# Products with the values emitted a step behind the transposes, and one ring of four banks for scores and transposes

## The chip, the cores and the metric

The kernel runs on one core of a Trainium2 chip. The time is that of the device for one whole execution, in microseconds, and the measure of a version is the median of its runs.

## The reference, cut to what matters

One decoder block over 2048 tokens of width 1024, all in float32. A modulated RMS norm is followed by one input projection, whose columns feed two head groups: four heads of chunked gated linear attention (GLA) and four heads of differential attention. Both groups' outputs go through one output projection (`w_out`), a norm and a residual; then comes a squared-ReLU MLP of width 4096 with the same frame. The change lies around the differential attention, whose core is this:

```python
    for blk in range(seq // Q_BLOCK):                       # 128 queries a block
        s = jnp.einsum('bhmqd,bhmkd->bhmqk', qb, kb) * scale   # m: two maps a head
        p = jax.nn.softmax(jnp.where(mask, s, -jnp.inf), axis=-1)
        p_diff = p[:, :, 0] - lam * p[:, :, 1]
        outs.append(jnp.einsum('bhqk,bhkd->bhqd', p_diff, vf[:, :, :q1]))
    ...
    do = from_heads(rms_norm(do, diff_norm) * (1.0 - lambda_init))
    return jnp.concatenate([go, do], axis=-1) @ w_out
```

## The kernel before

**Stages.** From 0 to about 667 us the kernel computes the norm, the input projections and the GLA chunks. Attention over the first 1024 queries (tiles t = 0 and 1 of 512 tokens) runs from about 667 to 892 us, at first between the last projections; attention over t = 2 and 3 from about 897 to 1300 us, with the output projection between its steps. From about 1345 us to the end the MLP runs.

**A step of attention.** `attention` is a generator over steps (t, h, j): tile, head, block of 128 queries. A step has one tick (one `yield`) for each 512 keys, so t + 1 ticks. In a tick, `qk(cur, ci)` issues for both maps two matmuls into a PSUM bank S (L209), and VectorE moves each bank to SBUF while it keeps a running minimum (L214, or L217 for the masked block). After the ticks, `softmax(cur)` takes two exponentials on ScalarE (L227) and one combination of the two maps on VectorE (L233). Two steps later (`lag` 2) come, in the same ticks, the products with the values, `pv(old, ci)`: up to four transposes of P into a bank PT (L248), one copy of the bank to SBUF by ScalarE (L250), and the matmuls of the copy with V into the head's bank O (L252), two instructions for each block of keys. After a head's last step, `finish` takes the norm of O (squares L262 on ScalarE, L264 and L266 on VectorE), transposes the result into a bank `dps` (L269), splits it (L271, L272) and stores it to `mixS`.

**Banks.** PSUM has eight banks in this pool: two each for the tags A (projections, Y), B (scores S; GLA's `sps`), C (PT, `dps`, transposes of other parts) and D (O).

**What lies between.** `interleave` runs the output projection between ticks: 1.5 to 2 sub-steps of three matmuls Y (L873 to L875) for each tick, as far as the tokens' heads are in `finished`. `prep_first` prepares the MLP's first operands in the same way (`ntr`, L923). The weights `w_out` are loaded in eight pieces by POOL (L850) into the three slots of tag `wx`, and each is split into two by ScalarE (L853) and VectorE (L854), after two ticks of attention for each piece. The tokens' x (L866) use the same slots later.

**Order.** Each engine runs its instructions in an order that is settled when the program is built: a scheduler takes, of what its own model of time holds to be ready, that which comes first in the program. So instructions can stand ahead of others that the program has before them. K, V and q are loaded by SP (L185, L187, L197), up to two steps ahead.

Of the kernel before, what the change touches and what calls it, by code (L numbers as in the profile page):

```python
# [9 lines left out]
F32 = mybir.dt.float32  # L10
# [4 lines left out]
ALU = mybir.AluOpType  # L15
# [4 lines left out]
P = 128  # L20
S = 2048
D = 1024
NK = D // P
NH = 4
# [25 lines left out]
def tile_hybrid_block(  # L50
# [3 lines left out]
    nc = tc.nc  # L54
# [95 lines left out]
    def modulate(xts, a1, sh, hi, lo, tp, ttag, tb, pp, ptags):  # L150

        for k in range(NK):
            ps = pp.tile([P, 512], F32, tag=ptags[k % len(ptags)], name="ntr", bufs=2)
            for i in range(4):
                nc.tensor.transpose(ps[:, i * P:(i + 1) * P], xts[i][:, k * P:(k + 1) * P], ident)
            hf = tp.tile([P, 512], F32, tag=ttag, name="nhf", bufs=tb)
            nc.scalar.activation(hf, ps, AF.Identity, bias=sh[:, k:k + 1], scale=a1[:, k:k + 1])
            nc.vector.tensor_copy(hi[:, k, :], hf)
            eng = nc.gpsimd if k % 2 else nc.vector
            eng.tensor_tensor(lo[:, k, :], hf, hi[:, k, :].bitcast(F32), op=ALU.subtract)  # L160


    finished = set()


    def attention(tlist, sb, pw, pb, pp, tags, kb_, vb_, lag):
# [69 lines left out]
                rsd[t, h] = sb.tile([P, 4], F32, tag="rsd", name="rsd", bufs=3)  # L236
            nc.vector.tensor_copy(rsd[t, h][:, j:j + 1], sums[:, 1, 0:1])

        def pv(step, g):
            t, h, j = step  # L240
            pd, Vc = tiles[step][0][0], heads[t, h][1]
            if (t, h) not in outs:
                outs[t, h] = pp.tile([P, 4, P], F32, tag=tags["O"][0], name="O", bufs=tags["O"][1])
            nb = 4 * t + j + 1
            kbs = range(4 * g, min(4 * g + 4, nb))
            tp = pp.tile([P, 4, P], F32, tag=tags["T"][0], name="PT", bufs=tags["T"][1])
            for kb in kbs:
                nc.tensor.transpose(tp[:, kb % 4, :], pd[:, kb * P:(kb + 1) * P], ident)  # L248
            pt = sb.tile([P, 4, P], F32, tag="PTs", name="PTs", bufs=3)
            nc.scalar.copy(pt[:, 0:len(kbs), :], tp[:, 0:len(kbs), :])  # L250
            for kb in kbs:
                nc.tensor.matmul(outs[t, h][:, j, :], pt[:, kb % 4, :], Vc[g][:, kb % 4, :], start=(kb == 0),  # L252
                                 stop=(kb == nb - 1))

        def finish(t, h):

            finished.add((t, h))
            ops, rs1 = outs.pop((t, h)), rsd.pop((t, h))
            ss = sb.tile([P, 4], F32, tag="dss", name="dss", bufs=2)
            for j in range(4):  # L260
                junk = sb.tile([P, P], BF16, tag="djunk", name="djunk", bufs=1)
                nc.scalar.activation(junk, ops[:, j, :], AF.Square, scale=rs1[:, j:j + 1], accum_out=ss[:, j:j + 1])  # L262
            rr = rsqrt_col(sb, ss, 4, 1.0 / P, "dr")
            nc.vector.tensor_tensor(rr, rr, rs1, op=ALU.mult)  # L264
            on = sb.tile([P, 4, P], F32, tag="don", name="don", bufs=1)
            nc.vector.tensor_tensor(on, ops, rr.unsqueeze(2).broadcast_to([P, 4, P]), op=ALU.mult)  # L266
            gps = pp.tile([P, 4, P], F32, tag=tags["T"][0], name="dps", bufs=tags["T"][1])
            for j in range(4):
                nc.tensor.transpose(gps[:, j, :], on[:, j, :], ident)  # L269
            mo = sb.tile([P, 4, 2, P], F32R, tag="dmo", name="dmo", bufs=1)  # L270
            nc.scalar.activation(mo[:, :, 0, :], gps, AF.Copy, scale=gnc[:, 1:2])  # L271
            nc.vector.scalar_tensor_tensor(mo[:, :, 1, :], gps, gnc[:, 1:2], mo[:, :, 0, :].bitcast(F32),  # L272
                                           op0=ALU.mult, op1=ALU.subtract)
            nc.gpsimd.dma_start(mixS[t][:, :, NH + h, :, :], mo.bitcast(F32))

        n = len(steps)
        for s in range(n + lag):
            cur = steps[s] if s < n else None
            old = steps[s - lag] if s >= lag else None
            if cur is not None:  # L280
                for a in range(3):
                    load(steps[min(s + a, n - 1)])
                tiles[cur] = ([sb.tile([P, pw], F32, tag="P", name="P", bufs=pb) for _ in range(2)],
                              [sb.tile([P, 4], F32, tag="nm", name="nm", bufs=8) for _ in range(2)],
                              sb.tile([P, 2, 2], F32, tag="sums", name="sums", bufs=4))
            nq = cur[0] + 1 if cur is not None else 0
            np_ = old[0] + 1 if old is not None else 0
            for ci in range(max(nq, np_)):
                if ci < nq:
                    qk(cur, ci)  # L290
                if ci < np_:
                    pv(old, ci)
                yield
            if cur is not None:
                softmax(cur)
            if old is not None:
                del tiles[old]
                if old[2] == 3:
                    finish(old[0], old[1])

# [133 lines left out]
    run(sh_a, 3)  # L436
    xts = load_x(0)
    run(sh_a)
    norm_in(0, xts, "CBDCBDCB")

    def gla_consts(pool, lraw):

# [144 lines left out]
    def gla_mix(qd, kdT, AT, gv, state, tag):  # L587

        ops = pp.tile([P, NH, P], F32, tag=tag, name="ops", bufs=2)
        for j in range(2):  # L590
            for hh in range(2):
                nc.tensor.matmul(ops[:, 2 * j + hh, :], qd[j], state[:, j, hh, :], start=True, stop=False)
                nc.tensor.matmul(ops[:, 2 * j + hh, :], AT[:, j, hh, :],
                                 gv[:, (2 * j + hh) * P:(2 * j + hh + 1) * P], start=False, stop=True)
        ups = pp.tile([P, 2, 2, P], F32, tag="C", name="ups", bufs=2)
        for j in range(2):
            nc.tensor.matmul(ups[:, j, :, :], kdT[:, j * P:(j + 1) * P], gv[:, 256 * j:256 * j + 256],
                             start=True, stop=True)
        return ops, ups
# [11 lines left out]

    def gla_store(ck, onm, sog, pool):
        on, mf = onm[:, 0, :, :], onm[:, 1, :, :]
        gps = pp.tile([P, NH, P], F32, tag="C", name="gps", bufs=2)
        for h in range(NH):
            nc.tensor.transpose(gps[:, h, :], on[:, h, :], ident)
        nc.vector.scalar_tensor_tensor(mf, gps, gnc[:, 0:1], sog, op0=ALU.mult, op1=ALU.mult)
# [5 lines left out]
    def gla(ts2):  # L623

        states = glac[3]
        for ck in range(4 * ts2[0], 4 * ts2[0] + 8):
            t, ci = ck // 4, ck % 4
            cs = slice(ci * P, (ci + 1) * P)
            gv, sog = gla_in(ck, sg, 2)
            tps = pp.tile([P, 256], F32, tag="C", name="tps", bufs=2)  # L630
            for j in range(2):
                nc.tensor.transpose(tps[:, j * P:(j + 1) * P], Ei[t, j][:, cs], ident)
            kdT = sg.tile([P, 256], F32, tag="kdT", name="kdT", bufs=2)
# [1 line left out]

            AT = sg.tile([P, 2, 2, P], F32, tag="AT", name="AT", bufs=2)
            for hh in range(2):
                sps = pp.tile([P, 2, P], F32, tag="B", name="sps", bufs=2)
                r = slice(64 * hh, 64 * hh + 64)
                for j in range(2):  # L640
                    nc.tensor.matmul(sps[:, j, :], Ei[t, j][r, cs], E[t, j][r, cs], start=True, stop=True)
                nc.vector.tensor_tensor(AT[:, :, hh, :], sps, tri.unsqueeze(1).broadcast_to([P, 2, P]), op=ALU.mult)
# [13 lines left out]
    def gla_any(tq, gn, gcon, masks):  # L656
# [20 lines left out]
        for ck in range(4 * tq, 4 * tq + 4):  # L677
# [1 line left out]
            gv, sog = gla_in(ck, gn, 1)  # L679
            AT = gn.tile([P, 2, 2, P], F32, tag="AT", name="AT")  # L680
            kdT = gn.tile([P, 256], F32, tag="kdT", name="kdT")
            tps = pp.tile([P, 256], F32, tag="C", name="tps", bufs=2)
            qd, eb = [], []
            for j in range(2):
                b = b16s[j][:, cs]

                def scores(qq, kk, mask, first):
                    for hh in range(2):
                        r = slice(64 * hh, 64 * hh + 64)
                        sps = pp.tile([P, P], F32, tag="B", name="sps", bufs=2)  # L690
                        nc.tensor.matmul(sps, kk[r], qq[r], start=True, stop=True)
                        if first:
                            nc.vector.tensor_tensor(AT[:, j, hh, :], sps, mask, op=ALU.mult)
# [118 lines left out]

    cA = ExitStack()
    sa = cA.enter_context(tc.tile_pool(name="pA0", bufs=2, side="right", reuse_waits="tile"))
    atags = {"S": ("B", 2), "O": ("D", 2), "T": ("C", 2)}
    at = attention((0, 1), sa, 1024, 6, pp, atags, 3, 3, 2)
    while run(dp, 1):
        run(at, AT0)
# [24 lines left out]
    sw = c1.enter_context(tc.tile_pool(name="p1w", bufs=2, side="left", reuse_waits="tile"))  # L843
    gtg = sw.tile([P, D], F32, tag="gtg", name="gtg", bufs=1)
    nc.gpsimd.dma_start(gtg, gtS[0].partition_broadcast(P))
    wohi, wolo = [], []
    for k in range(NK):
        run(at, WL)
        raw = sw.tile([P, D], F32, tag="wx", name="woraw", bufs=3)
        nc.gpsimd.dma_start(raw, w_out[k * P:(k + 1) * P, :])  # L850
        wh = sw.tile([P, D], F32R, tag=f"wohi{k}", name="wohi", bufs=1)
        wl = sw.tile([P, D], F32R, tag=f"wolo{k}", name="wolo", bufs=1)
        nc.scalar.copy(wh, raw)  # L853
        nc.vector.tensor_tensor(wl, raw, wh.bitcast(F32), op=ALU.subtract)  # L854
        wohi.append(wh)
        wolo.append(wl)

    def out_proj(tiles):

        for tk in tiles:  # L860
# [6 lines left out]
            yps = []  # L867
            ss = sw.tile([P, 2], F32, tag="wss", name="wss", bufs=2)
            for b in range(2):
                yp = pp.tile([P, 512], F32, tag=("B" if tk > 12 and tk % 2 else "A"), name="Y", bufs=2)  # L870
                cs = slice(512 * b, 512 * b + 512)
                for k in range(NK):
                    nc.tensor.matmul(yp, mx[:, k, 0, :], wohi[k][:, cs], start=(k == 0), stop=False)  # L873
# [34 lines left out]
    def prep_first(pool, tag):  # L908


        for n in range(16):
# [5 lines left out]
                nc.gpsimd.dma_start(raw[:, j], xnS[0][:, 4 * j + i].rearrange("p (e k) c -> p e k c", e=2)[:, :, k, :])  # L917
            for _ in range(3):
                yield
            ps = pp.tile([P, 2, 2, P], F32, tag=tag, name="ntr", bufs=2)  # L920
            for e in range(2):
                for j in range(2):
                    nc.tensor.transpose(ps[:, e, j, :], raw[:, j, e, :], ident)  # L923
# [577 lines left out]
```

## Time and profile before

| | |
|---|---|
| median of 3 runs | 2619.75 us (2618.13 to 2629.93) |
| the profiled execution | 2620.44 us |
| its span | 2618.7 us |
| TensorE matmul busy / weight loads busy | 95% / 78% of the span |
| VectorE / ScalarE / GpSimd busy | 61% / 44% / 17% |
| mean granted TensorE clock | 0.982 of full speed |

The profiled execution is 0.69 us above the median, and 1.7 us of it lie outside the span. TensorE has two rows: PE is the matmuls, whose ends are modelled, so that consecutive ones overlap in the trace; PEld is the weight load ahead of each. An idle time is put down to what released the instruction after it. "PEld O L252 <- ACT PTs L250" reads: the weight load of line 252, for the bank O, stood until ScalarE's copy of line 250 was done.

### The profile page before, as it was taken

Reading aid. Unit: us, or ns where it says so; the run is one execution under the profiler, and the core shown is the slowest. Engines: PE = TensorE matmul, PEld = TensorE weight load, DVE = VectorE, ACT = ScalarE, POOL = GpSimd, SP = SyncE. Lnnn points to the kernel's source line nnn. Section 1 sums busy time; section 2 is a strip of 40 time slices with the busy share of each in tenths; the row PEclk is TensorE's granted clock in tenths of the full one; section 3 lists DMA queues with packets and bytes.
Section 4 is the critical chain, followed back from the end, with each engine's and each line's share of the span. In section 5 each row is a group of like instructions: output and inputs, shape, how many; then the busy total and the mean of one; then the engine's idle time right before and its main releaser. Section 6 shows DMA issues by size and latency. Waiting matters only on the chain.

```text
span 2618.7 us, 35437 instructions
## 1 busy us (share of the span) xinstructions
PE 2482.6 (95%) x12532; PEld 2043.2 (78%) x12532; DVE 1595.4 (61%) x3111; ACT 1154.8 (44%) x2185; POOL 435.5 (17%) x642
## 2 busy tenths in 40 slices
PE   3999999999998899999999999999999999999998
PEld 2887787987787787787877878788888888788886
DVE  5545765247764766766568666866665435443756
ACT  3351224323444655565546454655454324222444
POOL 1211332102320113223002231121121000100000
PEclk9999999999999899999999999999999999999999
DMA  6354552344744756565376564654447857755856
GB/s 235 107 193 137 170 196 77 125 131 155 224 155 142 227 173 207 186 201 187 109 261 234 194 238 141 225 190 144 139 151 258 289 189 234 268 197 162 282 168 208
DMA packets 219898, 491.63 MB, mean 188 GB/s; under 512 B 25872, under 2 KB 79936, under 8 KB 218176
## 3 DMA queue, kind: packets, MB, share of 16 engines
q1 hardware_dynamic: 171504, 329.33, 39.8%
q0 software_dynamic: 48208, 159.95, 16.3%
q8 instruction: 101, 1.65, 0.3%
q14 instruction: 85, 0.70, 0.1%
HBM read 329.79 MB, written 159.39 MB: 187 GB/s over the span
## 4 chain that ended last, share of the span: by engine, by line
PE 33%; issue 20%; DMA 5%; POOL 5%; DVE 3%; ACT 2%; SPq 0%; POOLq 0%; DVEq 0%; ACTq 0%
PE dn L1361 6%; PE dn L1363 6%; PE dn L1362 6%; PE O L252 3%; PE S L209 3%; PE Y L873 1%; PE Y L875 1%; POOL uS L1121 1%; PE Y L874 1%; POOL uS L1152 1%; PE PT L248 1%; DMA mx<-mixS 1%; PE upY L1195 1%; PE upY L1194 1%; PE upY L1193 1%
## 5 line engine op out<-in xcount | busy, mean ns | idle before, releaser
L1361 PE MATMUL dn<-dnhi,uhi 128*128 128x512 f32 x880 | 344.2, 391 | 4.8 <-DVE du L1339 4.7
L1363 PE MATMUL dn<-dnhi,ulo 128*128 128x512 f32 x880 | 343.8, 391 | 0.1
L1362 PE MATMUL dn<-dnlo,uhi 128*128 128x512 f32 x880 | 343.8, 391 | 0.0
L1285 ACT CAST uhi<-us 128x1024 fp32r<-128x1024 f32 (+1 forms) x126 | 118.7, 944 | 352.6 <-PE dn L1362 325.8
L1287 DVE TENSOR_TENSOR ulo<-us,uhi 128x1024 fp32r<-128x1024 f32 (+1 forms) x126 | 137.0, 1087 | 152.6 <-ACT uhi L1285 149.9
L209 PE MATMUL S<-K,q 128*128 128x512 f32 (+3 forms) x640 | 193.9, 402 | 14.2 <-DVE P L214 7.5
L488 PE MATMUL projt<-hThi,whi 128*128 128x512 f32 x512 | 206.3, 403 | 0.6 <-DVE cols L370 0.3
L489 PE MATMUL projt<-hTlo,whi 128*128 128x512 f32 x512 | 205.9, 402 | 0.0
L490 PE MATMUL projt<-hThi,wlo 128*128 128x512 f32 x512 | 201.8, 394 | 2.1 <-DVE wlo L425 2.1
L1361 PEld LDWEIGHTS dn<-dnhi,uhi 128*128 128x128 f32 x880 | 165.7, 188 | 41.0 <-issue 5.1
L1363 PEld LDWEIGHTS dn<-dnhi,ulo 128*128 128x128 f32 x880 | 165.7, 188 | 35.7 <-DVE ulo L1287 0.6
L1362 PEld LDWEIGHTS dn<-dnlo,uhi 128*128 128x128 f32 x880 | 165.7, 188 | 35.1
L227 ACT ACTIVATE P<-P,nm 128x128 f32<-128x128 f32 (+15 forms) x128 | 153.8, 1203 | 65.2 <-DVE nm L217 59.7
L1075 ACT CAST wuhi<-wA 128x512 fp32r<-128x512 f32 x160 | 99.1, 619 | 162.7 <-PE upV L1194 67.2
L252 PEld LDWEIGHTS O<-V,PTs 128*128 128x128 f32 x1088 | 136.5, 193 | 33.4 <-ACT PTs L250 26.6
L252 PE MATMUL O<-V,PTs 128*128 128x128 f32 x1088 | 154.7, 285 | 7.3 <-ACT PTs L250 3.5
L1195 PE MATMUL upY<-hhi,wulo 128*128 128x512 f32 x384 | 151.0, 393 | 1.5 <-DVE wulo L1076 1.5
L1193 PE MATMUL upY<-hhi,wuhi 128*128 128x512 f32 x384 | 150.9, 393 | 0.0
L1194 PE MATMUL upY<-hlo,wuhi 128*128 128x512 f32 x384 | 150.9, 393 | 0.0
L502 PE MATMUL projn<-whi,hThi 128*128 128x256 f32 x512 | 147.2, 288 | 3.8 <-DVE cols L370 2.3
L209 PEld LDWEIGHTS S<-K,q 128*128 128x128 f32 x640 | 111.7, 197 | 48.8 <-DVE P L214 21.9
L503 PE MATMUL projn<-wlo,hThi 128*128 128x256 f32 x512 | 146.7, 287 | 0.0
(321 smaller groups left out, 5759.9 us busy)
## 6 DMA issues: line engine op xcount, KB each, us to landing
us<-uS SPq DMA_DIRECT2D x94, 512.0 KB, 4.5
wA<-in_w_up_dram SPq DMA_DIRECT2D x128, 256.0 KB, 3.0
uS<-t POOLq DMA_DIRECT2D x128, 256.0 KB, 3.2
adaraw<-in_ada_w_dram SPq DMA_DIRECT2D x48, 512.0 KB, 4.4
wraw<-in_w_in_dram SPq DMA_DIRECT2D x48, 512.0 KB, 4.5
uS<-c POOLq DMA_DIRECT2D x96, 256.0 KB, 3.0
K<-kS SPq DMA_DIRECT2D x40, 512.0 KB, 4.6
wds<-in_w_down_dram SPq DMA_DIRECT2D x78, 256.0 KB, 4.3
```

The lines of the kernel that those rows point to most:

```text
L209: nc.tensor.matmul(ps[:, :wd], qt[:, m, hl, qs], Kc[ci][:, m, :wd], start=(hl == 0), stop=(hl == 1))
L227: nc.scalar.activation(Ps[m][:, :width], Ps[m][:, :width], AF.Exp, scale=-1.0, bias=nms[m][:, t:t + 1], accum_out=sums[:, 0, m:m + 1])
L252: nc.tensor.matmul(outs[t, h][:, j, :], pt[:, kb % 4, :], Vc[g][:, kb % 4, :], start=(kb == 0), stop=(kb == nb - 1))
L488: nc.tensor.matmul(ps, whi[k][:, cs], hi[:, k, :], start=(k == 0), stop=False)
L489: nc.tensor.matmul(ps, whi[k][:, cs], lo[:, k, :], start=False, stop=False)
L490: nc.tensor.matmul(ps, wlo[k][:, cs], hi[:, k, :], start=False, stop=(k == NK - 1))
L1193: nc.tensor.matmul(ps, whi[:, k, :], hi[:, k, :], start=(first and k == 0), stop=False, skip_group_check=not first)
L1194: nc.tensor.matmul(ps, whi[:, k, :], lo[:, k, :], start=False, stop=False, skip_group_check=not first)
L1195: nc.tensor.matmul(ps, wlo[:, k, :], hi[:, k, :], start=False, stop=(k == 3), skip_group_check=not first)
L1361: nc.tensor.matmul(banks[t], uhi[:, tk], whi, start=first, stop=False, skip_group_check=on)
L1362: nc.tensor.matmul(banks[t], uhi[:, tk], wlo, start=False, stop=False, skip_group_check=on)
L1363: nc.tensor.matmul(banks[t], ulo[:, tk], whi, start=False, stop=last, skip_group_check=on)
```

## The change

`pv` is taken apart. `turn` (transposes and copy) stays where `pv` was; the products are put into a list and emitted one tick later, between that tick's `qk` and `turn`. A head's norm follows its last product (`norm`), and `finish` (transposes, split, store) comes two ticks after that. When the steps are over, further ticks empty the list. The scores and the transposes share tag C, which now has four banks; tag B is gone, and what used it (GLA's `sps`, the norm's transposes at the start, some late Y) takes C. The first three pieces of `w_out` are loaded ahead of the loop, and piece k + 3 behind the split of piece k.

```diff
-        def pv(step, g):
+        queue, tick = [], [0]
+        def later(n_, f, *a):
+            queue.append((tick[0] + n_, f, a))
+        def due():
+            for e in [e for e in queue if e[0] <= tick[0]]:
+                queue.remove(e)
+                e[1](*e[2])
+        def turn(step, g):
             t, h, j = step
...
             nc.scalar.copy(pt[:, 0:len(kbs), :], tp[:, 0:len(kbs), :])
+            later(1, pv, step, g, kbs, pt, heads[t, h][1])
+
+        def pv(step, g, kbs, pt, Vc):
...
             for kb in kbs:
                 nc.tensor.matmul(outs[t, h][:, j, :], pt[:, kb % 4, :], Vc[g][:, kb % 4, :], start=(kb == 0),
                                  stop=(kb == nb - 1))
-        def finish(t, h):
-            finished.add((t, h))
+            if j == 3 and kbs[-1] == nb - 1:
+                norm(t, h)
+        def norm(t, h):
...
             nc.vector.tensor_tensor(on, ops, rr.unsqueeze(2).broadcast_to([P, 4, P]), op=ALU.mult)
+            later(2, finish, t, h, on)
+        def finish(t, h, on):
+            finished.add((t, h))
...
             for ci in range(max(nq, np_)):
+                tick[0] += 1
                 if ci < nq:
                     qk(cur, ci)
+                due()
                 if ci < np_:
-                    pv(old, ci)
+                    turn(old, ci)
                 yield
...
-                if old[2] == 3:
-                    finish(old[0], old[1])
+        while queue:
+            tick[0] += 1
+            due()
+            yield
...
-                sps = pp.tile([P, 2, P], F32, tag="B", name="sps", bufs=2)
+                sps = pp.tile([P, 2, P], F32, tag="C", name="sps", bufs=4)
...
-    atags = {"S": ("B", 2), "O": ("D", 2), "T": ("C", 2)}
+    atags = {"S": ("C", 4), "O": ("D", 2), "T": ("C", 4)}
...
+    def load_wo(k):
+        raw = sw.tile([P, D], F32, tag="wx", name="woraw", bufs=3)
+        nc.gpsimd.dma_start(raw, w_out[k * P:(k + 1) * P, :])
+        woraw.append(raw)
+    for k in range(3):
+        load_wo(k)
     for k in range(NK):
         run(at, WL)
-        raw = sw.tile([P, D], F32, tag="wx", name="woraw", bufs=3)
-        nc.gpsimd.dma_start(raw, w_out[k * P:(k + 1) * P, :])
...
+        if k + 3 < NK:
+            load_wo(k + 3)
```

## Rows read from the trace of the kernel before

**Rows 1.** The page's first part: busy time, share of the span, instructions.
```profile
PE 2482.6 (95%) x12532; PEld 2043.2 (78%) x12532; DVE 1595.4 (61%) x3111; ACT 1154.8 (44%) x2185; POOL 435.5 (17%) x642
```

**Rows 2.** Stretches of the attention: start and end, length, busy time of each engine (instructions), granted clock, share of the DMA engines, GB/s.
```profile
667.00:750.00 83.00, 78.81 (x422) 63.58 (x420) 66.13 (x206) 45.36 (x131) 23.13 (x29) 1.00 0.67 209
836.00:912.00 76.00, 61.16 (x300) 46.85 (x301) 51.82 (x148) 45.47 (x100) 11.96 (x18) 0.82 0.75 237
912.00:1000.00 88.00, 87.30 (x506) 71.33 (x504) 62.38 (x182) 48.76 (x105) 15.44 (x18) 1.00 0.54 176
1000.00:1100.00 100.00, 94.09 (x540) 75.41 (x540) 72.40 (x215) 58.44 (x121) 32.63 (x41) 1.00 0.62 201
1100.00:1200.00 100.00, 95.94 (x581) 80.43 (x581) 68.25 (x191) 57.49 (x108) 29.49 (x36) 0.97 0.61 197
1200.00:1293.00 93.00, 90.96 (x564) 76.00 (x563) 62.64 (x179) 55.94 (x106) 17.45 (x21) 1.00 0.41 133
```

**Rows 3.** Waits of the weight loads over the whole span: us in total, times, longest us.
```profile
PEld O L252 <- ACT PTs L250: 26.6, 87, 1.2
...
PEld S L209 <- DVE P L214: 21.9, 36, 2.4
...
PEld S L209 <- DVE nm L217: 12.2, 21, 3.0
...
PEld ops L593 <- DVE AT L642: 7.9, 9, 2.1
...
PEld dps L269 <- issue: 6.1, 7, 4.3
...
PEld dps L269 <- PE S L209: 2.4, 4, 0.9
```

**Rows 4.** Waits of the matmuls over the whole span, same columns.
```profile
PE Y L873 <- DMA mx<-mixS: 11.4, 2, 7.1
...
PE S L209 <- DVE P L214: 7.5, 12, 2.1
PE S L209 <- DVE nm L217: 5.6, 6, 2.6
PE dps L269 <- DVE don L266: 5.2, 3, 4.2
...
PE O L252 <- ACT PTs L250: 3.5, 10, 0.8
...
PE PT L248 <- DMA K<-kS: 0.5, 1, 0.5
```

**Rows 5.** Groups by line in 912 to 1293 us: line, engine, operation, out<-in, shapes, count; busy us, mean ns of one; idle us before them and what ended it.
```profile
L250 ACT COPY PTs<-PT 128x512 f32<-128x512 f32 (+2 forms) x108 | 56.6, 533 | 78.6 <-PE PT L248 78.5
L214 DVE TENSOR_SCALAR_CACHE_REDUCE P<-S,nm 128x512 f32<-128x512 f32 x92 | 67.5, 746 | 20.2 <-PE S L209 19.8
L233 DVE SCALAR_TENSOR_TENSOR P<-P,cf 128x1280 f32<-128x1280 f32 (+7 forms) x31 | 58.8, 1898 | 0.0
L227 ACT ACTIVATE P<-P,nm 128x1408 f32<-128x1408 f32 (+7 forms) x60 | 99.0, 1651 | 29.2 <-DVE nm L217 29.1
```

**Rows 6.** One wait of the products in order of time: start, us, engine, line, operation, count, in brackets the idle time before it and its releaser.
```profile
1079.11 0.63 PE L209 MATMUL S<-K,q 128*128 128x512 f32 x2
...
1079.84 0.56 ACT L250 COPY PTs<-PT 128x512 f32<-128x512 f32 x1
...
1080.45 0.97 PEld L252 LDWEIGHTS O<-V,PTs 128*128 128x128 f32 x8 [1.15 <-ACT PTs L250]
1080.45 1.16 PE L252 MATMUL O<-V,PTs 128*128 128x128 f32 x8 [0.71 <-ACT PTs L250]
```

**Rows 7.** One wait of the scores, same columns.
```profile
1095.31 2.08 DVE L233 SCALAR_TENSOR_TENSOR P<-P,cf 128x1792 f32<-128x1792 f32 x1
...
1095.58 0.50 PE L209 MATMUL S<-K,q 128*128 128x384 f32 x2
...
1097.38 0.74 DVE L214 TENSOR_SCALAR_CACHE_REDUCE P<-S,nm 128x512 f32<-128x512 f32 x1
...
1098.18 2.13 PE L209 MATMUL S<-K,q 128*128 128x384 f32 x5 [2.10 <-DVE P L214]
```

**Rows 8.** POOL's loads of `w_out` in order of time.
```profile
837.47 1.69 POOL L850 DMA_DIRECT2D woraw<-in_w_out_dram  x3 [0.35 <-PE S L209]
849.17 0.53 POOL L850 DMA_DIRECT2D woraw<-in_w_out_dram  x1 [10.01 <-DVE sums L230]
...
854.76 0.55 POOL L850 DMA_DIRECT2D woraw<-in_w_out_dram  x1 [2.20 <-DVE wolo L854]
859.41 0.53 POOL L850 DMA_DIRECT2D woraw<-in_w_out_dram  x1 [4.10 <-ACT PTs L250]
```

**Rows 9.** ScalarE's and VectorE's first and second split of `w_out`, in order of time.
```profile
846.57 1.04 ACT L853 CAST wohi<-woraw 128x1024 fp32r<-128x1024 f32 x1 [5.47 <-DMA woraw<-in_w_out_dram]
...
847.65 1.23 DVE L854 TENSOR_TENSOR wolo<-woraw,wohi 128x1024 fp32r<-128x1024 f32 x1 [4.91 <-ACT wohi L853]
...
853.25 1.22 DVE L854 TENSOR_TENSOR wolo<-woraw,wohi 128x1024 fp32r<-128x1024 f32 x1
```

**Rows 10.** A load queue's own waits, 660 to 1310 us: the V loads (L187) on products.
```profile
SPq L187 <- PE O L252: 74.6, 11, 22.8
```

More of the change, by code (lines that the diff above doesn't have):

```diff
@@ L152, in modulate @@
         for k in range(NK):
-            ps = pp.tile([P, 512], F32, tag=ptags[k % len(ptags)], name="ntr", bufs=2)
+            ps = pp.tile([P, 512], F32, tag=ptags[k % len(ptags)], name="ntr",
+                         bufs=4 if ptags[k % len(ptags)] == "C" else 2)
             for i in range(4):
@@ L237, in softmax @@
             nc.vector.tensor_copy(rsd[t, h][:, j:j + 1], sums[:, 1, 0:1])
-        def pv(step, g):
+        queue, tick = [], [0]
[6 more added lines that the diff above has]
+        def turn(step, g):
             t, h, j = step
-            pd, Vc = tiles[step][0][0], heads[t, h][1]
-            if (t, h) not in outs:
-                outs[t, h] = pp.tile([P, 4, P], F32, tag=tags["O"][0], name="O", bufs=tags["O"][1])
+            pd = tiles[step][0][0]
             nb = 4 * t + j + 1
@@ L250, in pv @@
             nc.scalar.copy(pt[:, 0:len(kbs), :], tp[:, 0:len(kbs), :])
+            later(1, pv, step, g, kbs, pt, heads[t, h][1])
+        def pv(step, g, kbs, pt, Vc):
+            t, h, j = step
+            nb = 4 * t + j + 1
+            if (t, h) not in outs:
+                outs[t, h] = pp.tile([P, 4, P], F32, tag=tags["O"][0], name="O", bufs=tags["O"][1])
             for kb in kbs:
@@ L438, in tile_hybrid_block @@
     run(sh_a)
-    norm_in(0, xts, "CBDCBDCB")
+    norm_in(0, xts, "CCDCCDCC")
     def gla_consts(pool, lraw):
@@ L594, in gla_mix @@
                                  gv[:, (2 * j + hh) * P:(2 * j + hh + 1) * P], start=False, stop=True)
-        ups = pp.tile([P, 2, 2, P], F32, tag="C", name="ups", bufs=2)
+        ups = pp.tile([P, 2, 2, P], F32, tag="C", name="ups", bufs=4)
         for j in range(2):
@@ L613, in gla_store @@
         on, mf = onm[:, 0, :, :], onm[:, 1, :, :]
-        gps = pp.tile([P, NH, P], F32, tag="C", name="gps", bufs=2)
+        gps = pp.tile([P, NH, P], F32, tag="C", name="gps", bufs=4)
         for h in range(NH):
@@ L629, in gla @@
             gv, sog = gla_in(ck, sg, 2)
-            tps = pp.tile([P, 256], F32, tag="C", name="tps", bufs=2)
+            tps = pp.tile([P, 256], F32, tag="C", name="tps", bufs=4)
             for j in range(2):
@@ L681, in gla_any @@
             kdT = gn.tile([P, 256], F32, tag="kdT", name="kdT")
-            tps = pp.tile([P, 256], F32, tag="C", name="tps", bufs=2)
+            tps = pp.tile([P, 256], F32, tag="C", name="tps", bufs=4)
             qd, eb = [], []
@@ L689, in scores @@
                         r = slice(64 * hh, 64 * hh + 64)
-                        sps = pp.tile([P, P], F32, tag="B", name="sps", bufs=2)
+                        sps = pp.tile([P, P], F32, tag="C", name="sps", bufs=4)
                         nc.tensor.matmul(sps, kk[r], qq[r], start=True, stop=True)
@@ L845, in tile_hybrid_block @@
     nc.gpsimd.dma_start(gtg, gtS[0].partition_broadcast(P))
-    wohi, wolo = [], []
+    wohi, wolo, woraw = [], [], []
+    def load_wo(k):
[4 more added lines that the diff above has]
+        load_wo(k)
     for k in range(NK):
         run(at, WL)
-        raw = sw.tile([P, D], F32, tag="wx", name="woraw", bufs=3)
-        nc.gpsimd.dma_start(raw, w_out[k * P:(k + 1) * P, :])
         wh = sw.tile([P, D], F32R, tag=f"wohi{k}", name="wohi", bufs=1)
         wl = sw.tile([P, D], F32R, tag=f"wolo{k}", name="wolo", bufs=1)
-        nc.scalar.copy(wh, raw)
-        nc.vector.tensor_tensor(wl, raw, wh.bitcast(F32), op=ALU.subtract)
+        nc.scalar.copy(wh, woraw[k])
+        nc.vector.tensor_tensor(wl, woraw[k], wh.bitcast(F32), op=ALU.subtract)
         wohi.append(wh)
         wolo.append(wl)
+        if k + 3 < NK:
+            load_wo(k + 3)
     def out_proj(tiles):
@@ L869, in out_proj @@
             for b in range(2):
-                yp = pp.tile([P, 512], F32, tag=("B" if tk > 12 and tk % 2 else "A"), name="Y", bufs=2)
+                yp = pp.tile([P, 512], F32, tag=("C" if tk > 12 and tk % 2 else "A"), name="Y",
+                             bufs=4 if tk > 12 and tk % 2 else 2)
                 cs = slice(512 * b, 512 * b + 512)
@@ L919, in prep_first @@
                 yield
-            ps = pp.tile([P, 2, 2, P], F32, tag=tag, name="ntr", bufs=2)
+            ps = pp.tile([P, 2, 2, P], F32, tag=tag, name="ntr", bufs=4)
             for e in range(2):
```

## The prediction

> **What bounds the kernel now.** I read the page's first part, then the stretches of the attention, then the waits of TensorE by both its rows, and last the order of time around single waits. TensorE is the bound: its matmuls are busy 95% of the span, VectorE 61%, ScalarE 44% [rows 1]. The change touches the attention, and there the picture is the same: from 912 to 1293 us the matmul row is busy for 94% to 99% of each stretch, VectorE for 67% to 72%, ScalarE for 55% to 60% [rows 2]. So what can be won is idle time of TensorE that a wait causes, and nothing else counts. Who causes it is seen in the waits: products that stand for ScalarE's copy, scores that stand for VectorE to empty a bank, and `dps` transposes that stand for the head's norm [rows 3, 4].
>
> How much idle time that is depends on the row that is read. The products' wait for the copy is 26.6 us in 87 waits by the weight loads and 3.5 us in 10 by the matmuls [rows 3, 4]. One wait shows why: the last scores begin at about 1079.3 us (two issued from 1079.11, ends modelled to 1079.74), the products at 1080.45; the matmul row counts 0.71 us, the load row 1.15 us [rows 6]. The truth lies between, since a matmul's modelled end covers idle time and a load runs ahead of its matmul anyway. I take the middle of both rows throughout: 15 us for the products, and (34.1 + 13.1) / 2 = 23.6 us for the scores [rows 3, 4].
>
> The Trainium skill (Perfetto Trace Analysis, Identifying the Most-Contended Engine) says that matmul busy time is no measure of TensorE's headroom and that the busy share of weight loads is to be read. Here the two are 95% and 78% [rows 1], so the trace agrees that they differ; by that rule alone the products' term below would be 20 us in place of 11, by the matmul row alone 3 us.
>
> **The change part by part.**
>
> *Products a tick later.* Nothing is added: the same transposes, copies and products. What moves is the order. A copy takes 0.53 us [rows 5], and it was late because it stood behind an exponential of 1.65 us [rows 5] or behind the small operations of a norm. In the wait shown the copy began at 1079.84 and the products stood right behind the scores [rows 6]. With a tick between them (381 us from 912 to 1293 for some 112 ticks of t = 2 and 3, so 3.4 us each [rows 2]) a copy has 3.4 us, more than one exponential plus its own 0.53 us, a little less than two exponentials and the copy (3.8 us). So most of these waits go, and those behind both exponentials of a step stay in part. I take three quarters of 15 us: -11 us. Bounds: -26.6 us (the load row, all gone) and 0.
>
> What is late next: O is done a tick later, and with it V's slots. V's loads wait for products already, 74.6 us in 11 waits on SP's queue [rows 10], and K and q loads stand behind them on that queue. A tick later is 3.4 us. It costs nothing, because TensorE waited only 0.5 us for such a load in the whole kernel [rows 4], and V's slots and V's need move by the same tick.
>
> *One ring of four banks.* Before, a score bank of a tick needs the same map's bank of the tick before. In a ring in program order (S, S, PT, S, S, PT) the first score of a tick takes the bank of a PT two ticks old, the second that of the tick's-before first score, and the PT that of its second score. So scores gain about one emptying of 0.75 us (L214) [rows 5], and transposes now depend on VectorE. The scores' waits are 57 with 34.1 us by the load row, 0.6 us each, but the largest are 2.4 and 3.0 us [rows 3]: one behind a combination L233 of 2.08 us stood 2.10 us and would still stand some 1.4 us [rows 7]. I take a quarter of 23.6 us: -6 us; bounds 0 and -34.1 us.
>
> *Transposes behind VectorE.* A cost that before cannot show. The nearest row is the combination L233, 1.90 us, 31 of them in 912 to 1293 us [rows 5]: it delays the emptying of both score banks. The transposes come after some 0.9 us of products in the tick, so full exposure is about 1.0 us for each, 31 us in all; none if VectorE has caught up. I take 3 us, near the low end, since VectorE is idle for more than a quarter of these stretches [rows 2].
>
> *Norm and `dps`.* The `dps` transposes stand 5.2 us by the matmul row, of which one wait is 4.2 us [rows 4]. That one is at the end of the first attention, where nothing else is left to issue; emitting it two ticks later there only adds empty ticks. The rest goes: -1 us; bounds 0 and -8.5 us (both rows of `dps` in [rows 3]).
>
> *Ticks that empty the list.* The last products, norm and `finish` come in ticks without scores. The chain from the last O to the store has the same length; Y sub-steps get ahead of it. +1 us, bounds 0 and +4 us, the size of the one such wait now [rows 4].
>
> *`w_out`.* In the trace three loads go at once at 837.47 us, and the later ones as soon as a slot is free: the fifth at 854.76, when the second split (from 853.25 for 1.22 us) is over [rows 8, 9]. The slots stay three, so a load for piece k + 3 can't go before the split of piece k, in either version. ScalarE's 5.47 us for the first piece [rows 9] is the transfer's own time among others, in the stretch with the low clock of 0.82 [rows 2]; its issue can't move. 0 us; bounds -2 us (what the later loads were late together, about half a microsecond each) and +2 us.
>
> *GLA's `sps`, the first norm, late Y.* Same eight banks, other names. GLA's products wait 7.9 us for AT, a VectorE result and not a bank [rows 3]. 0 us; bounds -4 and +4 us, half that row either way.
>
> Sum: -11 - 6 + 3 - 1 + 1 = -14 us against the profiled execution of 2620.44 us, so 2606.4 us. That execution is 0.7 us above the median of the runs, so I say 2606 us, 0.5% below the median. A measurement of this kernel can tell about 0.5%, 13 us, from no change: 2606.6 to 2632.9 us counts as the same.
>
> **The rivals.**
>
> *The order was already so.* The scheduler is free to put other work ahead of products that are not ready, and did: by the matmul row only 3.5 us of the products' waits are idle time [rows 4]. What goes there may come back as waits for score banks, since VectorE is the next to be late (34.1 us by the load row [rows 3]). For it: a wait is 0.3 us on the mean (26.6 / 87). Against it: those of 1.2 us are plain idle time [rows 3]. Then the products give -3, the ring -3, transposes +2: about -4 us, 2616 us. Chance 0.28.
>
> *The ring holds up the transposes (the other side).* TensorE's matmuls run one behind the other, so a transpose that lacks a bank holds up products, scores and Y behind it. The place is the tick after each combination L233. At the full 1.0 us for each of 31 it costs 31 us against gains of 17 us (11 + 6): +14 us, 2634 us. It decides from 17 / 31 = 0.55 us for each. Against it: the ring also frees a score. Chance 0.15. The Trainium skill (PSUM - Partial Sum Buffer, Engine vs sequencer instructions) has the rule that matmuls start and complete in program order; the trace agrees, as the one late score above stopped every matmul for 2.10 us [rows 7].
>
> *Short stops lower the clock.* The granted clock was 0.82 in the stretch with the long idle times and 0.97 to 1.00 elsewhere [rows 2]. If stops at shared banks brought a tenth of the 381 us to half speed, that would add 38 us to what is left of the gain: 2630 us or more. Chance 0.03. The Trainium skill (TensorE: Matmul & The Clock Gate, A second HAM failure mode: psum-queue depth-cycling) describes a kernel that cycled through banks and lost its clock so; the trace is against it so far, since scores and transposes rotate through two banks each at a granted 1.00.
>
> *All of it goes.* If both rows' upper ends are nearer the truth, the products give -20, the scores -12, with +3 and -1 as above: -30 us, 2590 us. Chance 0.08.
>
> **How the numbers follow.** The forecast (-14 us, own range 2597 to 2613 us) has a chance of 0.46; the rest as above. The forecast and "all of it" lie below 2606.6 us for the most part, "already so" and the upper part of the forecast within 0.5%, the other two mostly above. Faster 0.47, same 0.39, slower 0.14. The range takes the forecast, "already so" and the near part of both wings: 2594 to 2624 us.
>
> **What would show it.** In the changed kernel's waits "O <- ACT PTs" should fall from 26.6 us to under 8 us by the load row, the scores' two rows from 34.1 us to about 25 us, and `dps` to the one wait at the first attention's end. The three loads of `w_out` still go together, and ScalarE still waits some 5 us for the first. A new row "PT <- DVE P" of over 17 us would show the ring holding up the transposes. Wrong I would be most easily by the scheduler: it orders every engine anew, and the stretch from 836 to 912 us, where TensorE is busy for 61 of 76 us [rows 2] and Y stands 7.1 us for a transfer [rows 4], can move by some us either way for reasons that no term here has.

## The result and the profile after

The changed kernel takes 2601.05 us, the median of five runs (2595.49 to 2604.45), beside 2620.83 us for the kernel before on the same chip (2618.13 to 2629.93): a ratio of 0.9911, with 0.9893 to 0.993 as its interval, 0.9% faster. The predicted 2606 us lies 5 us above it. The profiled execution took 2595.49 us, its span 2593.8 us, against 2618.7 us before.

The work is the same and TensorE is still the bound. The first part of the page, to be held against [rows 1]:

```profile
PE 2465.0 (95%) x12532; PEld 2051.2 (79%) x12532; DVE 1592.9 (61%) x3111; ACT 1148.3 (44%) x2185; POOL 435.6 (17%) x642
```

Where the time went is seen by following the same matmul through both traces. The first scores of t = 2 begin at 897.1 us before and 889.9 us after (7 us gained by then), the last scores of all at 1282.0 and 1254.8 us (27 us), the end of the span differs by 25 us. So 20 us lie between those two marks, in attention over t = 2 and 3. That stretch, before and then after: start and end, length, busy time of PE, PEld, DVE, ACT and POOL (instructions), granted clock, DMA share, GB/s:

```profile
897.00:1282.00 385.00, 370.93 (x2144) 301.58 (x2143) 272.09 (x787) 220.96 (x439) 97.25 (x120) 0.97 0.57 187
```

```profile
890.00:1255.00 365.00, 352.08 (x2135) 304.49 (x2133) 271.11 (x787) 218.34 (x437) 97.21 (x120) 0.99 0.61 196
```

The weight loads are busy as long as before (302 and 304 us), and so are VectorE and ScalarE. The matmul row, with the same matmuls, is 19 us less "busy". Its idle time hardly fell (14 to 13 us): the modelled ends of the matmuls had covered the rest. The idle time that was won is seen in the load row alone, 83 us before (385.00 - 301.58) and 61 us after.

Which waits those were, in the same stretch, by the weight loads; first before:

```profile
PEld O L252 <- ACT PTs L250: 19.1, 65, 1.2
PEld S L209 <- DVE P L214: 18.2, 30, 2.4
PEld S L209 <- DVE nm L217: 6.0, 12, 3.0
```

and after:

```profile
PEld O L270 <- ACT PTs L261: 7.0, 16, 1.6
PEld Y L910 <- DVE wyt L923: 3.5, 2, 2.6
PEld dps L293 <- DVE don L285: 3.3, 2, 2.4
PEld Y L910 <- DMA mx<-mixS: 3.0, 1, 3.0
PEld S L210 <- DVE P L215: 1.8, 5, 0.5
PEld S L210 <- ACT PTs L261: 1.5, 3, 0.6
```

The products' waits fell from 19.1 to 7.0 us, the scores' from 24.2 to 3.3 us; Y and `dps`, some 10 us, are what is late next. Over the whole span, to be held against [rows 3] for the loads:

```profile
PEld O L270 <- ACT PTs L261: 15.8, 40, 1.6
...
PEld dps L293 <- issue: 10.0, 4, 6.6
...
PEld dps L293 <- DVE don L285: 3.8, 3, 2.4
...
PEld S L210 <- ACT PTs L261: 2.3, 6, 0.6
PEld S L210 <- DVE P L215: 2.1, 6, 0.5
```

and against [rows 4] for the matmuls:

```profile
PE dps L293 <- DVE don L285: 11.9, 6, 6.5
...
PE O L270 <- ACT PTs L261: 5.1, 11, 1.4
```

What the new order looks like is plain in two ticks of the matmul row (start, us, engine, line, operation, count):

```profile
1003.36 1.09 PE L210 MATMUL S<-K,q 128*128 128x512 f32 x4
1004.28 1.05 PE L270 MATMUL O<-V,PTs 128*128 128x128 f32 x8
1005.17 0.60 PE L259 MATMUL PT<-ident,P 128*128 128x128 f32 x4
1005.52 0.47 PE L910 MATMUL Y<-wohi,mx 128*128 128x512 f32 x1
...
1006.99 1.08 PE L210 MATMUL S<-K,q 128*128 128x512 f32 x4
1007.91 1.05 PE L270 MATMUL O<-V,PTs 128*128 128x128 f32 x8
1008.80 0.38 PE L259 MATMUL PT<-ident,P 128*128 128x128 f32 x2
```

Four scores, eight products, four transposes, six Y, and again, 3.6 us a tick without a stop: the order of the program. In the wait shown before, the products stood right behind two scores, and the copy that they need began only at 1079.84 us, 0.1 us after the modelled end of those scores [rows 6]. ScalarE had this exponential ahead of it:

```profile
1077.98 1.67 ACT L227 ACTIVATE P<-P,nm 128x1664 f32<-128x1664 f32 x1
```

### The profile page after: what moved, and what is told of

Read it like the earlier page. It is cut to its first block, busy times and chain, and to the rows that moved or that the text cites. A ratio compares the mean times of both kernels' runs of the same rounds, so it can differ in the third digit from the quotient of the medians.

```text
span 2593.8 us, 35416 instructions
## 1 busy us (share of the span) xinstructions
PE 2465.0 (95%) x12532; PEld 2051.2 (79%) x12532; DVE 1592.9 (61%) x3111; ACT 1148.3 (44%) x2185; POOL 435.6 (17%) x642
## 4 chain that ended last, share of the span: by engine, by line
issue 31%; PE 25%; POOL 6%; DMA 3%; DVE 2%; ACT 2%; POOLq 0%; SPq 0%; DVEq 0%; ACTq 0%
PE dn L1398 4%; PE dn L1400 4%; PE dn L1399 4%; PE S L210 2%; PE O L270 2%; POOL uS L1158 2%; POOL uS L1189 1%; PE Y L912 1%; PE Y L910 1%; PE Y L911 1%; PE PT L259 1%; POOL wdS L1277 1%; PE upY L1231 1%; PE upY L1230 1%; PE upY L1232 1%
## 5 line engine op out<-in xcount | busy, mean ns | idle before, releaser
L210 PE MATMUL S<-K,q 128*128 128x512 f32 (+3 forms) x640 | 169.7, 384 | 2.4 <-SPq L852 1.1
L270 PEld LDWEIGHTS O<-V,PTs 128*128 128x128 f32 x1088 | 140.8, 192 | 26.8 <-ACT PTs L261 15.8
L532 PE MATMUL projn<-whi,hTlo 128*128 128x256 f32 x512 | 147.1, 287 | 0.0
```

Of the source, the lines that this page charges most:

```text
L210: nc.tensor.matmul(ps[:, :wd], qt[:, m, hl, qs], Kc[ci][:, m, :wd], start=(hl == 0), stop=(hl == 1))
```

## The experiments

The change has four edits that can be made one without the other: the ring of four banks, the products a tick later, `finish` two ticks later (both through the list), and the order of `w_out`'s loads. The first three were run in all eight combinations. In the table a time is the ratio's distance from 1 times 2621 us; a ratio stands against the kernel before on the same chip. Two things hang on these edits besides. Every version with the list emits the norm with a head's last product, ahead of the next softmax, where the kernel before and the ring alone have it behind; so the rows differ in the norm's place too, and no run takes it apart. And `finish` is also what lets the output projection use a head, so later transposes mean that this comes later.

| ring | products later | `finish` later | ratio (interval) | us |
|---|---|---|---|---|
| - | - | - | 1 | 0 |
| yes | - | - | 1.0071 (1.0043 to 1.0098) | +19 |
| - | yes | - | 0.9966 (0.9948 to 0.9984) | -9 |
| - | - | yes | 1.0068 (1.0038 to 1.0097) | +18 |
| yes | yes | - | 1.0009 (0.9994 to 1.0025) | +2 |
| yes | - | yes | 1.0039 (1.0021 to 1.0058) | +10 |
| - | yes | yes | 0.9929 (0.9901 to 0.9957) | -19 |
| yes | yes | yes | 0.9924 (0.9898 to 0.9951) | -20 |
| all, with `w_out`'s order | | | 0.9911 (0.9893 to 0.993) | -23 |

**`w_out`'s loads alone.**

```diff
+    for k in range(3):
+        load_wo(k)
     for k in range(NK):
         run(at, WL)
-        nc.gpsimd.dma_start(raw, w_out[k * P:(k + 1) * P, :])
...
+        if k + 3 < NK:
+            load_wo(k + 3)
```

> Only w_out's loads are emitted three pieces ahead of their split; all else as before. By the prediction: no change, 2618 to 2622 us, the first three loads at once and ScalarE's wait for the first piece near 5 us. By the rival that the loads came late: up to 6 us faster.

Measured: 2619.61 us, 0.9994 (0.9978 to 1.0011). The term of nothing holds: here, too, the three loads go at once and ScalarE stands 4.54 us for the first piece. In the trace of the whole change the three loads go together and the first split stands for the transfer, as in [rows 8, 9] (in brackets the engine's idle time and its releaser):

```profile
833.06 1.72 POOL L878 DMA_DIRECT2D woraw<-in_w_out_dram  x3 [0.35 <-PE S L210]
...
840.47 1.04 ACT L887 CAST wohi<-woraw 128x1024 fp32r<-128x1024 f32 x1 [1.45 <-DMA woraw<-in_w_out_dram]
```

From issue to split it is 7.4 us, 9.1 us before; ScalarE's idle time ahead of it is shorter (1.45 for 5.47 us) because it had other work for longer.

**The ring alone.**

```diff
-    atags = {"S": ("B", 2), "O": ("D", 2), "T": ("C", 2)}
+    atags = {"S": ("C", 4), "O": ("D", 2), "T": ("C", 4)}
...
-                sps = pp.tile([P, 2, P], F32, tag="B", name="sps", bufs=2)
+                sps = pp.tile([P, 2, P], F32, tag="C", name="sps", bufs=4)
```

> Only the banks are changed: scores, transposes and GLA's sps in one ring of four; the products stand right behind their copy as before, w_out's loads as before. By the prediction's sum the ring gives -6 us and costs +3 us on the transposes: 2614 to 2619 us. By the theory from the trace of the changed kernel, in which the scores' waits are all but gone, the ring is the larger part: 2601 to 2608 us. If the two edits need one another, about 2616 us.

Measured: 2639.77 us, slower by 19 us. The stretch from the first scores of t = 2 to the last scores:

```profile
905.00:1298.00 393.00, 367.75 (x2147) 304.29 (x2145) 273.87 (x791) 220.68 (x440) 97.37 (x121) 0.97 0.55 179
```

and its waits by the weight loads:

```profile
PEld O L253 <- ACT PTs L251: 22.2, 72, 1.6
PEld dps L270 <- DVE don L267: 19.3, 7, 5.0
PEld S L210 <- DVE P L215: 3.2, 8, 1.0
PEld PT L249 <- DVE P L234: 2.1, 1, 2.1
```

The time lies outside all three ranges. The scores' waits are nearly gone, as the ring should do it, and the transposes PT stand 2.1 us for VectorE's combination: neither of the two mechanisms that the prediction set against each other decides. What stands is a third, the norm's transposes. One of these waits in order of time:

```profile
1105.07 2.08 DVE L234 SCALAR_TENSOR_TENSOR P<-P,cf 128x1792 f32<-128x1792 f32 x1
...
1107.93 0.69 DVE L267 TENSOR_TENSOR don<-O,drr 128x512 f32<-128x512 f32 x1
...
1108.67 1.11 PE L270 MATMUL dps<-ident,don 128*128 128x128 f32 x4 [4.59 <-DVE don L267]
...
1109.44 2.05 PE L210 MATMUL S<-K,q 128*128 128x512 f32 x4
```

The head's norm ran behind a combination of 2.08 us on VectorE, and TensorE's fixed order had `dps` ahead of the next scores: 4.59 us in which TensorE did nothing. In the kernel before there was one such wait of 4.2 us [rows 4]; here twelve make 32.3 us by the matmul row of the whole span, about half of them (16.0 us) before this stretch. One thing is the ring's own: `dps` takes a bank of it, and at 852.47 us scores stood 5.1 us until VectorE had read such a bank.

**Products and `finish` later, without the ring.**

```diff
+            later(1, pv, step, g, kbs, pt, heads[t, h][1])
...
+            if j == 3 and kbs[-1] == nb - 1:
+                norm(t, h)
...
+            later(2, finish, t, h, on)
```

> Only the order of emission is changed: products a tick later, the head's norm and its transposes after that; banks two and two as before, w_out's loads as before. By the prediction's sum: -11 us, 2606 to 2611 us, with the scores' waits by the load row still near 34 us. If the ring is the larger part: 2611 to 2618 us. If the scheduler had the products late already: 2615 to 2621 us.

Measured: 2602.22 us, 0.9929, below all three ranges. Nearly the whole gain comes without the ring. The scores' waits did not stay near 34 us either: over the whole span they are 22.4 us, with their banks as before. The stretch, and its two largest waits by the loads:

```profile
889.00:1262.00 373.00, 357.75 (x2131) 304.54 (x2130) 274.09 (x791) 218.65 (x439) 97.49 (x121) 0.98 0.60 192
```

```profile
PEld S L209 <- DVE P L214: 16.4, 26, 3.4
PEld O L269 <- ACT PTs L260: 6.9, 20, 0.9
```

**The same with the ring** (both diffs above; the whole change but for `w_out`).

> The changed kernel with w_out's loads as in the kernel before, that is both the ring and the later products. If w_out's loads do nothing: the time of the changed kernel, 2598 to 2603 us. If they hold part of the gain: 2604 us or more.

Measured: 2601.78 us, 0.9924. The same stretch:

```profile
893.00:1259.00 366.00, 353.85 (x2136) 306.12 (x2135) 271.14 (x787) 218.36 (x437) 97.22 (x120) 0.98 0.61 195
```

Here the ring does win 7 us of the stretch (373 to 366) and takes most of the scores' waits away, but the stretch begins 4 us later, and the total is the same within a few us. Whether the ring is worth anything on top of the other two edits can't be told: the two intervals overlap almost wholly.

**`finish` two ticks later, alone.**

```diff
-            later(1, pv, step, g, kbs, pt, heads[t, h][1])
+            pv(step, g, kbs, pt, heads[t, h][1])
```

(against products and `finish` later)

> Banks two and two, products right behind their copy as before; only the head's norm is emitted with the last product and its transposes two ticks later. If the gain of the later order comes from the products: 2617 to 2623 us. If it comes from taking the transposes of a head's norm away from the place where they stop TensorE: 2602 to 2608 us.

Measured: 2642.42 us, slower by 18 us and outside both ranges. The products' and the scores' waits are about as before; new in the stretch, by the matmul row, is this one:

```profile
PE ntr L950 <- DMA xnq<-xnS: 14.4, 6, 5.5
```

`ntr` are the transposes of `prep_first`, and their operand is loaded by POOL. POOL's own order around the longest of the six waits:

```profile
1068.22 0.72 POOL L297 DMA_DIRECT2D mixS<-dmo  x1 [12.47 <-DVE dmo L295]
1070.29 0.56 POOL L962 DMA_DIRECT2D hS<-hBq  x1 [1.35 <-ACT hBq L954]
...
1079.02 1.42 POOL L944 DMA_DIRECT2D xnq<-xnS  x2 [5.00 <-DMA hS<-hBq]
```

followed on TensorE by

```profile
1086.60 0.45 PE L950 MATMUL ntr<-ident,xnq 128*128 128x128 f32 x1 [5.55 <-DMA xnq<-xnS]
```

POOL stood 12.47 us for the head's result, but the store behind that one was not ready either: it stood another 1.35 us for its own data. The load then stood 5.00 us until a store of hBq had landed, and TensorE's order had `ntr` ahead of everything else some 2 us after the load was issued. In the kernel before, POOL stands as long for such stores, while `ntr` stands 1.2 us in all:

```profile
POOL mixS L274 <- DVE wrw L127: 27.0, 2, 17.5
```

So the load that is late for its reader is shown; that the later store of the head's result makes it late is not, and why this build puts load and reader so close stays open.

**Products a tick later, alone.**

```diff
-            later(2, finish, t, h, on)
+            finish(t, h, on)
```

(against products and `finish` later)

> Banks two and two; products a tick later, but a head's norm, transposes and store at once behind its last product. If the gain comes from the products: 2602 to 2608 us. If from the later transposes of the norm: 2615 to 2623 us.

Measured: 2612.71 us, -9 us, between the two ranges. Over the whole span the products' waits by the load row are 21.4 us in 50, down from 26.6 us in 87 [rows 3].

**The ring with `finish` later, and the ring with products later.** Each is the ring's diff with one of the two above.

> Ring of four, products right behind their copy, the norm's transposes two ticks later. The ring alone took 2640 us, with 32 us of waits of these transposes by the matmul row. If these waits alone make it slow: 2606 to 2615 us, the waits at 12 us or less. If the ring needs the later products: 2625 us or more.

Measured: 2631.46 us, +10 us. The products wait as in the ring alone (31.8 us in 103 over the span, there 31.5 us in 100). The norm's transposes still stand 17.0 us by the matmul row, about half of the 32.3 us: those waits are part of what makes the ring slow, and not the whole.

> Ring of four, products a tick later, the norm's transposes at once. If the waits of these transposes make the ring slow whatever the products do: 2620 us or more, with over 25 us of them. If the later products are what the ring needs: 2600 to 2606 us.

Measured: 2623.38 us, +2 us. The waits of the norm's transposes are 26.3 us by the matmul row of the whole span, as the first case had it. From 890 to 1330 us the matmuls stand for the norm's transposes, behind four VectorE operations of their own and of other norms:

```profile
PE dps L293 <- DVE wqv L123: 5.7, 1, 5.7
PE dps L293 <- DVE wrw L126: 5.0, 1, 5.0
PE dps L293 <- DVE don L285: 4.2, 4, 3.1
...
PE dps L293 <- DVE wrr L129: 3.2, 1, 3.2
```

That is 18.1 us. With `finish` two ticks later as well it is 8.5 us in the same window, 6.5 of them at the end of the first attention, and over the whole span 11.5 in place of 26.3 us. The kernel is 22 us faster (+2 to -20): some 15 us of that, by the matmul row, can be this wait, and the rest is not traced to one.

**Is that the cause of the slow `finish`?** The transposes `ntr` were put five ticks behind their load in place of three, and the pause behind them shortened, first on `finish` later alone:

```diff
-            for _ in range(3):
+            for _ in range(5):
...
-            for _ in range(2):
+            for _ in range(1):
```

> As finish_only (2642 us; TensorE stood 14.4 us for loads of xnq ahead of the transposes ntr, in 6 waits), but prep_first emits those transposes five ticks behind their load instead of three. If it is that wait that makes the later norm alone slow: 2624 to 2632 us, with the ntr wait under 4 us. If any new order moves the time by such an amount: anything from 2605 to 2645 us, without relation to that wait.

Measured: 2622.47 us, 0.9995 (0.9984 to 1.0007), and of the wait there is left

```profile
PE ntr L950 <- DMA xnq<-xnS: 1.4, 1, 1.4
```

The same two numbers changed in the kernel before, where that wait is 1.2 us and there was nothing to win:

> The kernel before with the same edit to prep_first alone. It waits only 1.2 us for xnq, so the edit has nothing to win: 2617 to 2625 us. It shows how far a new order by itself moves the time: if by 10 us or more, the single edits' times say little about their mechanisms.

Measured: 2615.13 us, 0.9973 (0.9958 to 0.9987), -7 us. So if the edit is worth the same in both kernels, of the 19 us between `finish` later with and without it (+18 to -1) 7 come from the new order for reasons that no wait named here explains, and 12 remain for a wait that fell by 13.0 us (14.4 - 1.4). Then the wait is most of the cause; that the two add up is assumed, and the table above shows edits that don't. POOL stands 12.49 us for a store of a head's result in this run, too, with that wait gone. The control says how far a small difference can be trusted: an edit that should do nothing moved the time by 7 us, and the -9 us of the products alone are hardly more.

**The same on the changed kernel, and `finish` four ticks later there** (`later(2, finish, ...)` to `later(4, finish, ...)`).

> The changed kernel with the same edit to prep_first. It waits 0.8 us for xnq, so nothing is to be won: 2597 to 2605 us. If the changed kernel's time hangs on a lucky order: slower by 8 us or more.

Measured: 2600.14 us, 0.9911 (0.9884 to 0.9938).

> The changed kernel with a head's transposes of the norm four ticks after the norm instead of two. It still stands 11.9 us for them by the matmul row, of which one wait of 6.5 us is at the end of the first attention and stays. If the rest goes: 2595 to 2599 us. If the later store to mixS is then late for the output projection: 2602 to 2612 us.

Measured: 2599.29 us, 0.9914 (0.9881 to 0.9947). Neither differs from the change as it stands. In the second the `dps` waits fall from 11.9 to 7.5 us by the matmul row, 7.2 of them one wait at the end of the first attention, and `ntr` waits 8.1 us for its load where it waited 0.8 us: one reader's wait for another's.

## Why the prediction was right, and where it was not

**Right: the direction, the place and about the size.** -14 us were predicted and -20 to -23 us came, most of it in the attention over t = 2 and 3. It held that the products' waits were real idle time, and the rival "the order was already so" falls with that. For the scores' waits it is not shown: on top of the other edits the ring takes them from 22.4 us to 4.4 us, and the time is the same. "The ring holds up the transposes" falls: PT stood for VectorE's combination 3.2 us at most over the whole span by the load row, in any version with the ring, where 17 us was to decide. "All of it goes" (-30 us) asked for more than came, and its -12 us for the scores is not the quarter of the load row that the rest of the working takes; that would be 8.5 us.

**The products' term (-11 us) is right alone and wrong in company.** Alone it is -9 us, as the middle of both rows had it. But it is worth -17 us with the ring, -37 us with `finish` later, -30 us with both (differences of rows of the table). It is the one edit of the three that gains in every company. The waits by the load row were to fall under 8 us and stand at 15.8 us.

**The ring's term (-6 us) failed as a term.** The waits it is about fell much further than said, from 34.1 us to 4.4 us over the span by the load row where 25 us was the forecast. Still the ring alone cost 19 us, with products later 11 us more than without it; with `finish` later it is -8 us, and with both lags -1 us. What the prediction missed is that a wait removed in front of one reader is removed in an order that is fixed at the build: other instructions now stood at the front, and of those the norm's transposes were late. The prediction had the ring's risk at the wrong reader (PT), and no rival of it had `dps`. It did name the scheduler's new order as its likeliest failing, without a term for it.

**The norm's term (-1 us) was mis-sized by far.** It was priced by what `dps` waits for in the kernel before, 5.2 us. Moving `finish` is worth -10 us on top of products later, -9 us on top of the ring, -22 us on top of both, and +18 us alone. In the version with products and ring but an early `finish` it is 26.3 us of waits that the trace of before cannot show, because there these instructions stood elsewhere. `dps` did not fall to one wait: it is 11.9 us in six, 6.5 us of it at the first attention's end, where nothing else is left to issue.

**Why the sum came out near all the same.** Its terms don't add: alone the three make +19 - 9 + 18 = +28 us, together -20 us. So the nearness of the sum is luck: one term was too small in company, one did nothing that can be told, one had the wrong size, and the full change happens to leave an order without a new reader that is late by much. That the time after is no lucky order is supported by the two variants that disturb it and stay within 1 us or two of it. That each interaction has the named wait as its whole cause is not shown; the +10 us of ring and `finish` were not taken apart, nor was the norm's place, nor what makes the build choose one order or another.

**The measure.** Taking the middle of both rows gave a smaller sum than what came. For the same work the matmul row read 352 to 372 us in the stretch, the load row 302 to 306 us in the six versions for which the stretch was read; lengths of 365 to 405 us differ by the idle time of the load row. The Trainium skill (Perfetto Trace Analysis, Identifying the Most-Contended Engine) says to judge TensorE by the busy share of its weight loads and not by that of its matmuls, and these runs agree. By that row the products' term would have been -20 us, which is nearer to what this edit is worth in company (-17 to -37 us) and too much for it alone (-9 us), so neither row gives the worth of one wait.

**The clock** went the other way than the rival had it. Its dips in the stretch, before and after:

```profile
897.00:905.00 8.00, 6.90 (x21) 4.07 (x19) 4.91 (x16) 2.87 (x4) 2.23 (x4) 0.55 1.03 340
905.00:913.00 8.00, 7.74 (x24) 5.04 (x25) 6.51 (x19) 4.17 (x8) 0.00 (x0) 0.60 0.72 214
...
1080.00:1120.00 40.00, 36.25 (x207) 29.32 (x208) 28.09 (x82) 20.98 (x45) 10.44 (x13) 0.96 0.60 192
...
1160.00:1200.00 40.00, 37.14 (x234) 31.75 (x233) 24.48 (x67) 20.83 (x39) 11.15 (x14) 0.96 0.57 188
```

```profile
890.00:898.00 8.00, 7.53 (x27) 5.90 (x25) 6.71 (x23) 3.28 (x5) 2.23 (x4) 0.71 0.48 147
898.00:906.00 8.00, 5.63 (x20) 4.51 (x21) 3.96 (x14) 2.89 (x5) 0.00 (x0) 0.79 1.05 344
```

Length times what is missing from 1 is 10.0 us before (3.6 + 3.2 + 1.6 + 1.6) and 4.0 us after (2.3 + 1.7); so up to 6 of the stretch's 20 us are clock, an estimate from these rows. From 899 to 911 us before, and from 888 to 894 and 902 to 904 us after, the granted clock is 0.50, the lower of its two levels (1.2 GHz); outside the dips it is 1.00 (2.4 GHz). Ahead of the falls TensorE stood: its matmul row was busy for 0.27 us from 893 to 897 us before, and not at all from 886 to 888 and from 898 to 900 us after. So the first dip after begins 2 us ahead of the stretch, and about 1 of the 6 us is only that; why the dips after are the shorter stays open.

## What to carry to other kernels

Where each engine's order is fixed when the program is built, the waits in a trace belong to that order: removing one shows who stands next, so of several reorderings price each also in the company of the others, and ask of every short chain (a norm, a load that waits for a store to land) whether its reader would now be at the front. Read the idle time of a stretch of TensorE from the weight loads, and trust no difference from a reordering that is smaller than what a reordering without a purpose makes, 7 us here. What gained in every company here was to give the copies one whole tick between ScalarE and the products that read them; two ticks for the norm's transposes gained in three of four.

## What the runs showed that was not expected

A norm whose last operation takes 0.69 us (`don`) made TensorE stand 4.59 us, with scores that needed nothing from it behind its reader; single edits that add and remove no work moved the kernel by 18 and 19 us, as much as the whole change gained. And moving the transposes of a head's norm was felt in a part of the kernel that needs nothing from them, as loads that came too late for `ntr`: 14.4 us in six waits.
